# Padding on-chip tiles to 512-byte starts, and weights as the stationary operand in block 1's up projections

## The chip, the cores and the metric

The kernel runs on one core of a Trainium2 chip. The time is the device time of one execution in microseconds (us); the figure that counts is the median over several runs. TensorE (PE in the rows) multiplies: each product first loads a stationary operand of 128x128 numbers (a weight load, PEld in the rows) and then streams a moving operand of up to 512 columns through it into PSUM. VectorE (DVE), ScalarE (ACT) and GpSimd (POOL) do the elementwise work; SyncE (SP) issues the DMAs.

## The reference, cut to what matters

Two transformer-like blocks follow each other on 256 tokens with a width of 1024; a second stream of 256 context tokens joins in the second block.

```python
def swiglu(x, w_gate, w_up, w_down):
    return (jax.nn.silu(x @ w_gate) * (x @ w_up)) @ w_down
...
x = x + 0.5 * swiglu(rmsnorm(x, ffn1_norm[l]), ffn1_w_gate[l], ffn1_w_up[l], ffn1_w_down[l])
x = x + hybrid_mixer(rmsnorm(x, mix_norm[l]), ...)
x = x + 0.5 * swiglu(rmsnorm(x, ffn2_norm[l]), ffn2_w_gate[l], ffn2_w_up[l], ffn2_w_down[l])
...
mods = jnp.split(jax.nn.silu(c) @ w_ada[layer] + b_ada[layer], N_MOD, axis=-1)
h = ffn_sublayer(h, mods[0], mods[1], mods[2], ...)
hc = ffn_sublayer(hc, mods_c[0], mods_c[1], mods_c[2], ...)
...
h = ffn_sublayer(h, mods[6], mods[7], mods[8], ...)
```

The hidden width of every feed-forward part is 2816, which is 22 groups of 128 features. `w_ada` gives the nine modulation vectors of block 2.

## The kernel before, in words

Every float32 factor is split into a high and a low part (`split_out`): ScalarE rounds the high part, VectorE subtracts it from the source for the low part. A product of the reference is three products on TensorE (high x high, high x low, low x high), made by `mm3`, `mm3r`, `projT` or `projT2`, all through `mm` (line 79). So the whole kernel is a stream of about 7,000 products with one weight load each. The splits of a weight go from a tile `raw` (where the DMA lands it) to the tiles `wh` and `wl`; one such unit is 128x1024 numbers, 512 KB. Activations stand transposed in `XH` and `XL` (8 slices of 128 features, 512 tokens each) and hidden activations in slot tiles `S0` to `S17` (`salloc`).

The order of work is one queue per engine. The queues come out of a scheduler that keeps dependences and lets ready work of a later step go ahead; its results are seen in the program's order, shown below for the places of interest.

The four feed-forward parts in the order in which they run:

- Block 1's first and second (`ffn2tok` with `gu1`, `gu2`), on two tiles of 128 tokens. Eleven chunks `c` of 256 features: `proj_chunk` takes the activations as stationary and streams the weights, 512 columns (256 gate, 256 up), 48 products a chunk. `sink_gu` (line 336) makes the gated product on 128 tokens x 256 features; it is then transposed on TensorE (`later`, line 348) so that the down projection can take it as stationary. The RMS factor `r` of a token is a per-partition number here: it goes into the activation's `scale` and into the gated product. The down projection runs over 22 units of `Wd`, 12 products of 512 columns each.
- The context and the tokens of block 2 together (`ffn4tok`, `gu3`, 512 columns): weights stationary, `XH` and `XL` moving; 48 products for each of 22 feature groups, in two parts (12 and 10 groups), each with its down projection.
- Block 2's last (`ffn2tok` with `cols=True`, `gu4`): one chunk in the first form, then for each feature group `f` from 2 to 21 the weights are stationary and 256 columns of `XH` and `XL` move, 48 products a group; no transposes are needed.

Between these lie the two mixers.

Beside the up projections VectorE also makes the row sums of `w_ada` (`ada_gen`, line 543): 72 units of 512 KB are loaded, each is multiplied with `silu(c)` and summed, two such instructions for each of the first 40 units and one for each of the other 32. `self.fill_every` says after how many split units one step of that generator is put into the order.

All tiles lie in one address range of 128 partitions, in the order of the pools. From the sizes in the code the start of each tile within a partition follows; what stands here is its remainder modulo 512 bytes. Slices of a tile that are used as operands begin at multiples of 512 bytes from its start (exceptions: the 272- and 258-column operands of the mixers).

| tile | before | after the change |
|---|---|---|
| `ident` | 128 | 0 |
| `XH`, `XL` | 160 | 0 |
| `t2`, `x2`, `x3`, `bc` | 0 | 0 |
| `S0`, `S1` | 128, 160 | 0 |
| `S2`, `S3` | 192 | 0 |
| `S4` to `S7` | 224 | 0 |
| `S8` to `S12` | 256 | 0 |
| `S13` to `S17` | 288 | 0 |
| `wh`, `wl`, `raw` | 288 | 0 |

In the first part of `ffn4tok`, the first half of the down projection streams `wh` and `wl` against hidden activations in slots. Its third and fourth unit (24 products each) take them from `S13`, `S14`, `S16` and `S17`, the fifth and sixth from `S8` to `S11`.

Of the kernel before, what the change touches and what calls it, by code (L numbers as in the profile page):

```python
# [9 lines left out]
F32 = mybir.dt.float32  # L10
F32R = mybir.dt.float32r
# [12 lines left out]
class Kern:  # L24
    def __init__(self, tc, A, out, pools):
        self.tc, self.nc, self.A, self.out = tc, tc.nc, A, out
        self.__dict__.update(pools)
        self.n = 0
        self.free_slots = list(range(NSLOT))
        self.slot_of = {}  # L30
        self.filler = None
        self.fill_every = 0
        self.fill_count = 0
        self.filled = 0
        self.pre = []
        self.deferred = []
        self.later_pe = []
        self.held = 0


# [10 lines left out]
    def psum(self, tag, shape):  # L51
        return self.ps.tile(shape, F32, tag=tag, name=self.nm(tag), bufs=4)

    def salloc(self, shape, dt=F32):
        i = self.free_slots.pop(0)
        t = self.slots.tile(shape, dt, tag=f"S{i}", name=self.nm(f"S{i}"))
        self.slot_of[id(t)] = (i, t)
        return t
# [262 lines left out]
    def ffn2tok(self, Wgu, Wd, xts, rows, sink, after, skew=4, cols=False, first_by_tile=False, w0=(), fine=False, mid=None, ahead=None):  # L321


        hT = {}

        def dest(f):
# [5 lines left out]
        for c in range(1 if cols else 11):  # L332
            self.fill_every = 2 if self.filler is not None and 1 <= c < 10 else 0
            trs = []

            def sink_gu(t, ps, c=c, trs=trs):
# [4 lines left out]
                if r is None:  # L341
                    self.act(sil, ps[:, :256], AF.Silu)
                    self.tt(h, ps[:, 256:], sil, ALU.mult)
                else:
                    self.act(sil, ps[:, :256], AF.Silu, scale=r)
                    self.stt(h, ps[:, 256:], r, sil, ALU.mult, ALU.mult)

# [17 lines left out]
        if cols:  # L365
            toks = slice(xts[0][0] * P, xts[0][0] * P + 256)
            for f in range(2, NF):
                self.fill_every = 3 if self.filler is not None and f < 20 else 0
                ws = [self.unit(Wgu[2 * f + j]) for j in range(2)]
                pss = [self.psum("acc", [P, 256]) for _ in range(2)]  # L370
                self.projT2(pss, ws, toks)
                sil, h = self.t2([P, 256]), self.t2([P, 256])
                self.act(sil, pss[0], AF.Silu)
                self.tt(h, pss[1], sil, ALU.mult)
                hh, hl, sl = dest(f)
                self.split_out(hh[:, sl, :], hl[:, sl, :], h)
                if f == 2:
                    self.flush()
        if mid is not None:
            mid()  # L380
# [10 lines left out]

        for f in range(NF - skew):
            wh, wl = self.unit(Wd[f])
            hh, hl, sl = dest(f)
# [42 lines left out]
    def ffn4tok(self, Wgu, Wd, xts, sink, after, ws):  # L437

        u0 = 0
        for part, (f0, f1) in enumerate(((0, 12), (12, 22))):  # L440
# [28 lines left out]
            for f in range(f, f1):  # L469
                self.fill_every = 1 if f0 + 4 < f or f0 else 0  # L470
                ws = [self.unit(Wgu[2 * f + j]) for j in range(2)]
                pss = [self.psum("acc", [P, 512]) for _ in range(2)]
                self.projT2(pss, ws, slice(0, 512))
                sink_gu(f, *pss)
            self.fill_every = 0
            nu = (f1 - f0) // 2
            for d in range(2):
                pss = {}

# [624 lines left out]
    def run(self):  # L1104
        nc, A = self.nc, self.A
        x = {}
        for t in (2, 3):
            x[t] = self.xres.tile([P, D], F32, tag=f"x{t}", name=f"x{t}")
        self.ident = self.cpool.tile([P, P], F32, tag="ident", name="ident")
        make_identity(nc, self.ident)  # L1110
        g = {"f1": self.bc.tile([P, D], F32, tag="bc", name="bc_f1")}
# [8 lines left out]
        self.tri = self.cpool.tile([P, 2, P], F32, tag="tri", name="tri")  # L1120
        self.XH = self.cpool.tile([P, 8, 512], F32R, tag="XH", name="XH")
        self.XL = self.cpool.tile([P, 8, 512], F32R, tag="XL", name="XL")
        lat = (2, 3)

        def res_half(t, d, ps):
            s = slice(d * 512, d * 512 + 512)
            self.stt(x[t][:, s], ps, 0.5, x[t][:, s], ALU.mult, ALU.add)

# [29 lines left out]

        self.ffn2tok(A["gu1"], A["d1"], xts, rows, res_half, after)
        g["f2"] = self.bcast(A["ffn2_norm"])  # L1160
# [55 lines left out]

        self.ffn2tok(A["gu2"], A["d2"], xf, rf, res_half, after, mid=mid, ahead=ahead)

# [80 lines left out]
def body(tc, A, out):  # L1299
    with tc.tile_pool(name="const", bufs=1) as cpool, \  # L1300
# [10 lines left out]
        pools = dict(cpool=cpool, xres=xres, small=small, tmp=tmp, bc=bc, rp=rp, slots=slots, raw=raw, wsp=wsp, ps=ps)  # L1311
        k = Kern(tc, A, out, pools)
        k.modd = dram.tile([112, P], F32, tag="modd", name="modd")
        k.mrow = dram.tile([36, 256], F32, tag="mrow", name="mrow")
# [59 lines left out]
def layout(i):  # L1374
# [9 lines left out]
    a["g_final"] = i["g_final_2"].reshape(1, D)  # L1384
    a["gu1"] = pack_gu(i["ffn1_w_gate"][0], i["ffn1_w_up"][0])
    a["gu2"] = pack_gu(i["ffn2_w_gate"][0], i["ffn2_w_up"][0])
    a["gu3"] = pack_T(i["w_ffn1_in_2"][0]).reshape(2, NF, P, D).transpose(1, 0, 2, 3).reshape(2 * NF, P, D)
# [57 lines left out]
```

## Time and profile before

| what | us |
|---|---|
| median of 3 runs | 1427.51 (1427.47 to 1428.04) |
| the profiled execution | 1426.11 |
| its span, first to last instruction | 1424.3 |
| PE busy in it | 1404.2 (99%) |
| DVE busy | 919.5 (65%) |
| ACT busy | 626.5 (44%) |
| mean DMA rate | 183 GB/s |

A busy PE means that some product was in its pipeline at the time; products overlap, so the busy time of one instruction (some 395 ns for 512 columns) is longer than the distance from its start to the next one's. What a product costs is that distance: the difference of two start times divided by the number of products between. In a table of windows the number behind the x also counts instructions that began just before the window, so it is one or two above the number that starts in it.

### The profile page before, as it was taken

What the parts mean: (1) busy time and instruction counts of PE and PEld (TensorE: products, weight loads), DVE (VectorE), ACT (ScalarE), POOL (GpSimd) and SP (SyncE); (2) the same over time, 40 slices, a digit from 0 to 9 for tenths busy, and PEclk for the clock granted to TensorE, in tenths of its full rate; (3) what the DMA queues carried; (4) which work ended last, traced back from release to release, by engine and by line L of the source; (5) the groups of instructions that cost most, each with busy time, mean ns of one, the idle gap of its engine ahead of it and who ended that gap; (6) DMA issues with size and microseconds to landing.
All of it is one profiled execution on the core that took longest, in us unless ns stands there. A gap on an engine that the chain in (4) does not pass through costs nothing. (4 is left out here: it accounts for less than half of the span.)

```text
span 1424.3 us, 18795 instructions
## 1 busy us (share of the span) xinstructions
PE 1404.2 (99%) x7222; PEld 1170.0 (82%) x7222; DVE 919.5 (65%) x1308; ACT 626.5 (44%) x914; POOL 29.3 (2%) x49
## 2 busy tenths in 40 slices
PE   7999999999999999999999999999999999999997
PEld 5888788778888898888888887888988887899986
DVE  5998556878988475542555446476886566655545
ACT  5445447464446442322122224343865455444442
POOL 0000000000000000000000001001010000000000
PEclk9999999999999999999999999999999999999999
DMA  8888646457887664643565442333335666465662
GB/s 278 307 269 275 205 136 204 134 166 259 290 275 254 203 210 132 195 147 102 191 209 178 147 148 94 115 104 129 102 104 187 198 192 206 142 197 179 184 207 69
DMA packets 73307, 260.71 MB, mean 183 GB/s; under 512 B 8172, under 2 KB 9216, under 8 KB 73216
## 3 DMA queue, kind: packets, MB, share of 16 engines
q1 hardware_dynamic: 72928, 259.11, 56.3%
q8 instruction: 57, 0.93, 0.3%
q10 hardware_dynamic: 288, 0.39, 0.1%
q14 instruction: 34, 0.28, 0.1%
HBM read 258.32 MB, written 1.14 MB: 182 GB/s over the span
## 5 line engine op out<-in xcount | busy, mean ns | idle before, releaser
L69 DVE TENSOR_TENSOR wl<-raw,wh 128x1024 fp32r<-128x1024 f32 (+1 forms) x381 | 459.0, 1212 | 330.3 <-ACT wh L66 326.7
L66 ACT ACTIVATE wh<-raw 128x1024 fp32r<-128x1024 f32 (+1 forms) x381 | 398.3, 1049 | 609.0 <-PE acc L79 457.9
L79 PE MATMUL acc<-wh,XH 128*128 128x512 f32 (+2 forms) x816 | 277.3, 398 | 0.4 <-ACT t L66 0.4
L79 PE MATMUL acc<-wh,XL 128*128 128x512 f32 (+2 forms) x816 | 273.4, 393 | 0.2 <-DVE XL L69 0.2
L79 PE MATMUL acc<-wl,XH 128*128 128x512 f32 (+2 forms) x816 | 272.4, 392 | 0.0
L79 PE MATMUL acc<-wh,S 128*128 128x512 f32 x872 | 237.1, 394 | 0.4 <-DVE t L72 0.4
L79 PE MATMUL acc<-XH,wh 128*128 128x512 f32 (+1 forms) x776 | 201.5, 339 | 0.0
L79 PE MATMUL acc<-XH,wl 128*128 128x512 f32 (+1 forms) x776 | 201.2, 339 | 0.0
L79 PE MATMUL acc<-XL,wh 128*128 128x512 f32 (+1 forms) x776 | 201.1, 339 | 0.0
L79 PEld LDWEIGHTS acc<-wh,S 128*128 128x128 f32 x872 | 162.8, 188 | 38.8 <-DVE t L72 1.1
L543 DVE SCALAR_TENSOR_TENSOR S<-raw,S 128x1024 f32<-128x1024 f32 x112 | 136.9, 1222 | 70.6 <-DMA raw<-in_w_ada 69.9
L79 PEld LDWEIGHTS acc<-wh,XL 128*128 128x128 f32 x816 | 152.2, 189 | 34.6 <-DVE XL L69 1.1
L79 PEld LDWEIGHTS acc<-wl,XH 128*128 128x128 f32 x816 | 152.0, 188 | 33.7 <-DVE wl L69 0.3
L79 PEld LDWEIGHTS acc<-wh,XH 128*128 128x128 f32 x816 | 151.7, 189 | 33.9 <-ACT t L66 0.6
L79 PEld LDWEIGHTS acc<-XL,wh 128*128 128x128 f32 x776 | 133.0, 188 | 17.5
L79 PEld LDWEIGHTS acc<-XH,wl 128*128 128x128 f32 x776 | 132.9, 188 | 17.5
L79 PEld LDWEIGHTS acc<-XH,wh 128*128 128x128 f32 x776 | 132.9, 188 | 17.5
L79 PE MATMUL acc<-wl,S 128*128 128x512 f32 x436 | 133.0, 393 | 0.0
L79 PEld LDWEIGHTS acc<-wl,S 128*128 128x128 f32 x436 | 81.9, 188 | 18.4
L66 ACT ACTIVATE S<-t 128x512 fp32r<-128x512 f32 (+2 forms) x58 | 31.4, 542 | 30.2 <-DVE t L69 30.2
L66 ACT ACTIVATE XH<-tr 128x512 fp32r<-128x512 f32 x44 | 26.0, 596 | 41.8 <-PE tr L152 41.3
L152 PE MATMUL tr<-ident,t 128*128 128x128 f32 x200 | 32.1, 285 | 10.4 <-DVE t L69 9.6
(165 smaller groups left out, 892.9 us busy)
## 6 DMA issues: line engine op xcount, KB each, us to landing
raw<-in_gu SPq DMA_DIRECT2D x176, 512.0 KB, 4.4
raw<-in_d SPq DMA_DIRECT2D x88, 512.0 KB, 4.3
raw<-in_w_ada SPq DMA_DIRECT2D x72, 512.0 KB, 4.5
raw<-in_w_in SPq DMA_DIRECT2D x68, 512.0 KB, 4.3
raw<-in_w_qk SPq DMA_DIRECT2D x16, 512.0 KB, 3.5
bc<-modd SPq DMA_DIRECT2D x10, 512.0 KB, 4.4
raw<-in_w_out SPq DMA_DIRECT2D x8, 512.0 KB, 3.5
raw<-in_w_b SPq DMA_DIRECT2D x8, 512.0 KB, 4.3
```

What stands on the lines that cost most here:

```text
L66: return self.nc.scalar.activation(out=out, in_=in_, func=func, **kw)
L69: return self.nc.vector.tensor_tensor(out=out, in0=a, in1=b, op=op)
L79: self.nc.tensor.matmul(out, l, r, start=start, stop=stop, **kw)
L152: self.nc.tensor.transpose(tr[:, j, :], src[:, j * P:(j + 1) * P], self.ident)
L543: nc.vector.scalar_tensor_tensor(out=junk, in0=raw, scalar=1.0, in1=cb[r], op0=ALU.mult, op1=ALU.mult, accum_out=mc[:, o:o + 1])
```

## The change

It has four parts.

1. Pad tiles (`pad`) and a new order of the constant tiles; slot tiles that hold 4x258 numbers take 4608 bytes and not 4128. The table above gives the result.
2. Block 1's two feed-forward parts call `ffn2tok` with `cols=True`, and `layout` packs `gu1` and `gu2` accordingly. Chunk 0 keeps its form; the feature groups 2 to 21 have stationary weights and 256 moving columns. Tokens then lie along the columns, so `r` can no longer be a per-partition factor: four transposes build a tile `R` with `r` of each token in all partitions, VectorE multiplies the gate's sum by `R` ahead of the activation, and the factor of the up half is moved to the residual (`rhalf` is 0.5 times `r`).
3. Where the steps of `ada_gen` go: in block 1's up projections one after 4 units up to group 19 (first) or 15 (second), one after 2 units in the first down projection, and more of them in `ffn4tok`.
4. `res_half` takes `rhalf` in place of 0.5.

```diff
@@ salloc
+        if len(shape) == 3 and shape[1] * shape[2] > D:
+            t = self.slots.tile([P, D + P], dt, tag=f"S{i}", name=self.nm(f"S{i}"))
+            t = t[:, :shape[1] * shape[2]].rearrange("p (a b) -> p a b", a=shape[1])
@@ ffn2tok
+        R = self.salloc([P, 256]) if rows else None
...
-            self.fill_every = 2 if self.filler is not None and 1 <= c < 10 else 0
+            self.fill_every = 0
...
-                    self.stt(h, ps[:, 256:], r, sil, ALU.mult, ALU.mult)
+                    self.tt(h, ps[:, 256:], sil, ALU.mult)
...
+                def row():
+                    tr = self.psum("tr", [P, 256])
+                    for i in range(2):
+                        self.nc.tensor.transpose(tr[:, i * P:i * P + P], b[:, i * P:i * P + P], self.ident)
+                    self.act(R, tr)
+
+                self.after_mm(10, row)
...
-                self.fill_every = 3 if self.filler is not None and f < 20 else 0
+                self.fill_every = 4 if self.filler is not None and f < (16 if mid else 20) else 0
...
-                self.act(sil, pss[0], AF.Silu)
+                if rows:
+                    self.tt(sil, pss[0], R, ALU.mult)
+                    self.act(sil, sil, AF.Silu)
+                else:
+                    self.act(sil, pss[0], AF.Silu)
...
+            self.fill_every = 2 if self.filler is not None and not mid and f < NF - skew - 2 else 0
@@ ffn4tok
-                self.fill_every = 1 if f0 + 4 < f or f0 else 0
+                self.fill_every = 1 if f0 + 2 < f or f0 else 0
+                if f0 and f % 2 and self.filler is not None:
+                    next(self.filler, 0)
...
+                self.fill_every = 0 if part and d else 2
@@ run
+        self.pad(self.cpool, 96)
         self.ident = self.cpool.tile([P, P], F32, tag="ident", name="ident")
+        self.XH = self.cpool.tile([P, 8, 512], F32R, tag="XH", name="XH")
+        self.XL = self.cpool.tile([P, 8, 512], F32R, tag="XL", name="XL")
...
+        self.pad(self.cpool, 32)
...
-            self.stt(x[t][:, s], ps, 0.5, x[t][:, s], ALU.mult, ALU.add)
+            self.stt(x[t][:, s], ps, self.rhalf[t], x[t][:, s], ALU.mult, ALU.add)
...
-        self.ffn2tok(A["gu1"], A["d1"], xts, rows, res_half, after)
+        self.ffn2tok(A["gu1"], A["d1"], xts, rows, res_half, after, cols=True)
...
-        self.ffn2tok(A["gu2"], A["d2"], xf, rf, res_half, after, mid=mid, ahead=ahead)
+        self.ffn2tok(A["gu2"], A["d2"], xf, rf, res_half, after, cols=True, mid=mid, ahead=ahead)
@@ body
+        k.pad(rp, 64)
@@ layout
-    a["gu1"] = pack_gu(i["ffn1_w_gate"][0], i["ffn1_w_up"][0])
-    a["gu2"] = pack_gu(i["ffn2_w_gate"][0], i["ffn2_w_up"][0])
+    a["gu1"] = pack_guT(i["ffn1_w_gate"][0], i["ffn1_w_up"][0])
+    a["gu2"] = pack_guT(i["ffn2_w_gate"][0], i["ffn2_w_up"][0])
```

TensorE's queue in block 1's first up projection, before: the end of one chunk of 256 features, with the transposes (`tr`) of the chunk ahead, and the start of the next. `acc_257` and `acc_258` are the sums of the two token tiles; the operand behind the arrow is the moving one, then the stationary one.

```order
L79 MATMUL acc_258<-wl_304,XH 128x512
L353 MATMUL tr_319<-ident,t_37_238 128x128 x2
L353 MATMUL tr_319<-ident,t_39_248 128x128 x2
L79 MATMUL acc_257<-wh_330,XH 128x512
L79 MATMUL acc_257<-wl_331,XH 128x512
L79 MATMUL acc_257<-wh_330,XL 128x512
L79 MATMUL acc_257<-wh_330,XH 128x512
```

The same queue now, where one feature group ends and the next begins: `acc_368` and `acc_369` are the gate's and the up half's sums over both token tiles.

```order
L88 MATMUL acc_368<-XL,wh_346 128x256
L88 MATMUL acc_369<-XL,wh_352 128x256
L88 MATMUL acc_368<-XH,wl_347 128x256
L88 MATMUL acc_369<-XH,wl_353 128x256
L88 MATMUL acc_437<-XH,wh_427 128x256
L88 MATMUL acc_438<-XH,wh_433 128x256
L88 MATMUL acc_437<-XL,wh_427 128x256
```

Weights and activations have changed places, a product has 256 columns in place of 512, and no transpose stands between two groups.

VectorE's queue in the same up projection, before, for one chunk: four splits (`wl`), the low part of the transposed hidden activations (`S_101`), the two gated products (line 72) and four row sums (line 543).

```order
L69 TENSOR_TENSOR wl_557<-raw_554,wh_556 128x1024
L69 TENSOR_TENSOR S_101_521<-tr_515,S_100_520 128x512
L69 TENSOR_TENSOR wl_577<-raw_574,wh_576 128x1024
L72 SCALAR_TENSOR_TENSOR t_107_541<-acc_461,r_155,t_106_540 128x256
L543 SCALAR_TENSOR_TENSOR S_50_283,mc<-raw_580,S_48_277 128x1024
L72 SCALAR_TENSOR_TENSOR t_109_551<-acc_462,r_166,t_108_550 128x256
L543 SCALAR_TENSOR_TENSOR S_50_283,mc<-raw_580,S_49_280 128x1024
L69 TENSOR_TENSOR wl_599<-raw_596,wh_598 128x1024
L69 TENSOR_TENSOR wl_624<-raw_621,wh_623 128x1024
L543 SCALAR_TENSOR_TENSOR S_50_283,mc<-raw_627,S_48_277 128x1024
L543 SCALAR_TENSOR_TENSOR S_50_283,mc<-raw_627,S_49_280 128x1024
```

The same queue now, for two feature groups, which are as many features as a chunk: `S_31` is `R`, `acc_798` and `acc_867` are the gate's sums of the two groups, `t_140` and `t_150` what goes to the activation, `S_130` the low part of the hidden activations.

```order
L78 TENSOR_TENSOR t_140_848<-acc_798,S_31_184 128x256
L78 TENSOR_TENSOR wl_933<-raw_930,wh_932 128x1024
L78 TENSOR_TENSOR wl_1000<-raw_997,wh_999 128x1024
L78 TENSOR_TENSOR t_141_849<-acc_799,t_140_848 128x256
L78 TENSOR_TENSOR S_130_779<-t_141_849,S_129_778 128x256
L78 TENSOR_TENSOR t_150_917<-acc_867,S_31_184 128x256
L78 TENSOR_TENSOR wl_1006<-raw_1003,wh_1005 128x1024
L78 TENSOR_TENSOR t_151_918<-acc_868,t_150_917 128x256
L78 TENSOR_TENSOR wl_1071<-raw_1068,wh_1070 128x1024
L78 TENSOR_TENSOR S_130_779<-t_151_918,S_129_778 128x256
L577 SCALAR_TENSOR_TENSOR S_69_362,mc<-raw_1080,S_67_356 128x1024
L577 SCALAR_TENSOR_TENSOR S_69_362,mc<-raw_1080,S_68_359 128x1024
```

For the same features there are two row sums in place of four, and two more short instructions that read the gate's sum; one or two splits stand between that instruction and the gated product of the same group.

## Rows read from the trace of the kernel before

**Rows 1.** The page, part 1: busy time, share of the span, instructions.

```profile
span 1424.3 us, 18795 instructions
PE 1404.2 (99%) x7222; PEld 1170.0 (82%) x7222; DVE 919.5 (65%) x1308; ACT 626.5 (44%) x914; POOL 29.3 (2%) x49
```

**Rows 2.** Waits of TensorE: who for whom, us in total, times, longest.

```profile
PE tr L152 <- DVE t L69: 9.6, 3, 6.4
PE tr L152 <- DVE t L72: 0.8, 3, 0.4
```

**Rows 3.** TensorE's timeline in `ffn4tok`'s first down half: start, length, instructions (us).

```profile
657.95 2.00 PE L79 MATMUL acc<-wh,S 128*128 128x512 f32 x8
...
660.69 1.98 PE L79 MATMUL acc<-wh,S 128*128 128x512 f32 x8
...
663.41 1.98 PE L79 MATMUL acc<-wh,S 128*128 128x512 f32 x8
...
666.13 1.98 PE L79 MATMUL acc<-wh,S 128*128 128x512 f32 x8
...
668.86 2.03 PE L79 MATMUL acc<-wh,S 128*128 128x512 f32 x8
...
671.66 2.03 PE L79 MATMUL acc<-wh,S 128*128 128x512 f32 x8
...
674.46 0.39 PE L79 MATMUL acc<-wh,S 128*128 128x512 f32 x1
```

**Rows 4.** The same two stretches as windows: TensorE busy, granted clock, DMA.

```profile
657.95:668.86 10.91, 10.91 (x50) 1.00 0.32 96
668.86:680.06 11.20, 11.20 (x49) 1.00 0.30 94
```

**Rows 5.** Windows: first up projection; `ffn4tok`'s second; last `ffn2tok`'s (PE, PEld, DVE, ACT, POOL, clock, DMA).

```profile
36.00:108.00 72.00, 72.00 (x324) 58.21 (x323) 65.56 (x92) 34.15 (x44) 0.00 (x0) 1.00 0.86 289
713.33:825.32 111.99, 111.99 (x481) 90.10 (x480) 54.75 (x72) 29.67 (x38) 0.00 (x0) 1.00 0.53 172
1246.31:1354.61 108.30, 108.30 (x915) 108.30 (x914) 58.14 (x77) 51.29 (x78) 0.00 (x0) 1.00 0.61 188
```

**Rows 6.** TensorE's timeline around one chunk of the first up projection.

```profile
34.30 0.60 PE L353 MATMUL tr<-ident,t 128*128 128x128 f32 x4
34.65 0.47 PE L79 MATMUL acc<-wh,XH 128*128 128x512 f32 x1
...
45.92 0.60 PE L353 MATMUL tr<-ident,t 128*128 128x128 f32 x4
46.28 0.47 PE L79 MATMUL acc<-wh,XH 128*128 128x512 f32 x1
```

**Rows 7.** TensorE's groups with shapes kept apart: count, busy us, mean ns, idle before.

```profile
L79 PE MATMUL acc<-wh,XH 128*128 128x512 f32 x784 | 271.3, 402 | 0.4 <-ACT t L66 0.4
...
L79 PE MATMUL acc<-wh,S 128*128 128x512 f32 x872 | 237.1, 394 | 0.4 <-DVE t L72 0.4
L79 PE MATMUL acc<-wl,S 128*128 128x512 f32 x436 | 133.0, 393 | 0.0
L79 PE MATMUL acc<-XH,wh 128*128 128x512 f32 x392 | 123.8, 395 | 0.0
...
L79 PE MATMUL acc<-XH,wh 128*128 128x256 f32 x384 | 77.7, 282 | 0.0
```

**Rows 8.** VectorE's and ScalarE's groups, shapes kept apart, same columns.

```profile
L69 DVE TENSOR_TENSOR wl<-raw,wh 128x1024 fp32r<-128x1024 f32 x373 | 453.4, 1222 | 328.4 <-ACT wh L66 326.4 <-PE acc L79 1.0
L543 DVE SCALAR_TENSOR_TENSOR S<-raw,S 128x1024 f32<-128x1024 f32 x112 | 136.9, 1222 | 70.6 <-DMA raw<-in_w_ada 69.9
L543 DVE DVE_READ_ACCUMULATOR S<-raw,S 128x1 f32 x112 | 9.4, 84 | 0.0
L69 DVE TENSOR_TENSOR t<-acc,t 128x256 f32<-128x256 f32 x22 | 9.2, 419 | 1.0 <-ACT t L66 1.0
L66 ACT ACTIVATE t<-acc,r 128x256 f32<-128x256 f32 x46 | 20.3, 468 | 5.0 <-PE acc L79 5.0
```

More of the change, by code (lines that the diff above doesn't have):

```diff
@@ L38, in __init__ @@
         self.held = 0
+        self.rhalf = {}
     def nm(self, s):
@@ L52, in psum, with pad @@
         return self.ps.tile(shape, F32, tag=tag, name=self.nm(tag), bufs=4)
+    def pad(self, pool, n):
+        pool.tile([P, n], F32, tag=f"pad{n}", name=self.nm("pad"), bufs=1)
     def salloc(self, shape, dt=F32):
         i = self.free_slots.pop(0)
-        t = self.slots.tile(shape, dt, tag=f"S{i}", name=self.nm(f"S{i}"))
+        if len(shape) == 3 and shape[1] * shape[2] > D:
+            t = self.slots.tile([P, D + P], dt, tag=f"S{i}", name=self.nm(f"S{i}"))
+            t = t[:, :shape[1] * shape[2]].rearrange("p (a b) -> p a b", a=shape[1])
+        else:
+            t = self.slots.tile(shape, dt, tag=f"S{i}", name=self.nm(f"S{i}"))
         self.slot_of[id(t)] = (i, t)
@@ L366, in ffn2tok @@
             toks = slice(xts[0][0] * P, xts[0][0] * P + 256)
+            if rows:
+                b = self.t2([P, 256])
+                for i, (t, _) in enumerate(xts):
+                    self.ts(b[:, i * P:i * P + P], self.ident, 0.0, rows[t], ALU.mult, ALU.add)
+                    self.rhalf[t] = self.rp.tile([P, 1], F32, tag=f"h{t}", name=self.nm("h"))
+                    self.ts(self.rhalf[t], rows[t], 0.5)
+                def row():
[4 more added lines that the diff above has]
+                self.after_mm(10, row)
             for f in range(2, NF):
-                self.fill_every = 3 if self.filler is not None and f < 20 else 0
+                self.fill_every = 4 if self.filler is not None and f < (16 if mid else 20) else 0
                 ws = [self.unit(Wgu[2 * f + j]) for j in range(2)]
@@ L372, in ffn2tok @@
                 sil, h = self.t2([P, 256]), self.t2([P, 256])
-                self.act(sil, pss[0], AF.Silu)
+                if rows:
+                    self.tt(sil, pss[0], R, ALU.mult)
+                    self.act(sil, sil, AF.Silu)
+                else:
+                    self.act(sil, pss[0], AF.Silu)
                 self.tt(h, pss[1], sil, ALU.mult)
@@ L378, in ffn2tok @@
                     self.flush()
+        if rows:
+            self.sfree(R)
         if mid is not None:
@@ L474, in ffn4tok @@
                 sink_gu(f, *pss)
-            self.fill_every = 0
             nu = (f1 - f0) // 2
             for d in range(2):
+                self.fill_every = 0 if part and d else 2
                 pss = {}
@@ L1120, in run @@
         self.tri = self.cpool.tile([P, 2, P], F32, tag="tri", name="tri")
-        self.XH = self.cpool.tile([P, 8, 512], F32R, tag="XH", name="XH")
-        self.XL = self.cpool.tile([P, 8, 512], F32R, tag="XL", name="XL")
+        self.pad(self.cpool, 32)
         lat = (2, 3)
```

## The prediction

> **What bounds the kernel now.** The page's first part comes first: PE is busy for 99% of the span, VectorE for 65% [rows 1]. That alone proves little, because products overlap; the waits decide. All that TensorE waits for is a handful of moments, 9.6 us of them in three gaps at the start [rows 2]. So the span is about 7,000 products in a row, and the question is the distance from one start to the next.
>
> For 512 columns that distance is not one number. In the first down half of `ffn4tok` twelve products go from 657.95 to 660.69 us, 2.74 us, and again in 2.72, 2.72 and 2.73; from 668.86 on twelve take 2.80, twice [rows 3]. Over 48 products that is 10.91 / 48 = 227.3 ns, and over the next 48 it is 11.20 / 48 = 233.3 ns. [...] What differs is the slots: the fast 48 read stationary operands that begin at 288 bytes modulo 512, as their moving operands do; the slow 48 read them at 256. Elsewhere the two operands stand 128 apart (160 and 288), and there 480 products take 111.99 us, 233.3 ns each [rows 5]; in a chunk of the first up projection 48 take 11.27 us, 234.8 ns [rows 6]. So the distance depends on where operands lie, and equal remainders give the shortest one in this trace.
>
> **The change part by part.** The sum is made against the span of 1424.3 us.
>
> *Padding, 512 columns.* After it all these products have equal remainders (0 and 0), so each gets 227.3 ns, the price of the 48. Of the 4,884 products with 512 columns (the program's count; [rows 7] shows the groups: three of 784, three of 392, 872, 436, and 48 others), 1,056 are block 1's up projections, dealt with below. 1,308 are the down projections with slots (872 + 436): they run between 227.3 and 233.3 already, depending on the slot, so they get half the difference: 1,308 x 3.0 = 3.9 us. The other 2,520 stand 128 apart: 2,520 x 6.0 = 15.1 us. The bound on the other side is zero (rival B); that a start at 0 could be slower than 233.3 I leave out, because no pair of remainders in the trace is much slower than that (234.8 at most, [rows 6]).
>
> [...]
>
> *Padding, 256 columns.* 1,448 such products exist now. 912 of them take 108.30 us, 118.8 ns each [rows 5]; their operands stand 128 apart (160 and 288), and no 256-column product with equal remainders is in the trace. From above the price is 118.8, unchanged. From below: each product has one weight load whatever its width, so if the 6.0 ns belong to the load, 112.8 is left; if they belong to the columns, 118.8 x 227.3 / 233.3 = 115.7. I take 114, between these two and nearer to the first, since it was the stationary operand's place alone that changed within [rows 3]. 1,448 x 4.8 = 6.9 us.
>
> *Block 1's up projections.* A chunk takes 46.28 - 34.65 = 11.63 us, of which the four transposes are 0.36 [rows 6]. Twenty chunks (ten in each part; chunk 0 keeps its form) are 232.6 us. They become 40 groups of 48 products with 256 columns: 40 x 48 x 0.114 = 218.9 us. That saves 13.7 us: 7.2 are the transposes, the rest is what padding does. At the old 118.8 ns it would be 228.1, so 4.5 us saved. The two chunks 0 get 96 x 7.5 ns = 0.7 us. The four transposes for `R` cost 0.4 us.
>
> *VectorE beside it.* Now it is busy for 65.56 of 72 us in that stage [rows 5], 10.6 us of each 11.63. Per group it will do two splits of 1.222 us and three short instructions of 0.42 (product with `R`, gated product, low part) [rows 8]: 3.70 us. A step of `ada_gen` is two row sums, 2 x (1.222 + 0.084) = 2.61 us, once in two groups: 5.01 us against 48 x 0.114 = 5.47 of TensorE. I cost the new instruction at nothing, since this slack covers it; without the cover, 40 x 0.42 = 17 us. What is queued behind the multiplication with `R` when it waits for the gate's sum are the splits for later groups and the row sums. They are two groups ahead (five pairs of `wh` and `wl`), so a wait there reaches TensorE only after some 5 us.
>
> *Where the row sums go.* The first down projection gets one step after two units: 1.222 + 1.31 = 2.53 us of VectorE for 12 products, 2.73 us. That is 93%, and the cover is thin, but the up projections run at 91% now without TensorE waiting. Its DMA is 1.5 x 524 KB in 2.73 us, 288 GB/s, and 289 are carried in the up projection now at a share of 0.86 [rows 5]. In `ffn4tok` a group takes 10.9 us, and VectorE is busy for only 54.75 of 112 [rows 5]. These moves cost nothing. Nor do `rhalf` in place of 0.5 and the pads.
>
> Sum: 3.9 + 15.1 + 6.9 + 13.7 + 0.7 - 0.4 = 39.9 us. The span becomes 1384.4. The profiled execution took 1426.11 us, 1.8 above its span, and the median of the runs is 1427.51, 1.4 above that: 1427.5 - 39.9 = 1387.6, so 1388 us, 2.8% faster.
>
> **The rivals.**
>
> *A: the start address itself counts too.* The fast 48 have equal remainders, but their operands still cross a 512-byte boundary inside each slice; after the change none does. [...] Against it: operands with the same difference but other places cost about the same (chunks at 288 and 160, groups at 160 and 288, within 1.5 ns).
>
> [...]
>
> *B: the padding does not do what the 48 suggest.* The 227.3 could come from those slots or from that stretch, say from how the halves alternate. Then only the new form of the up projections counts: 4.5 - 0.4 = 4.1 us, 1423.4 us. For it: only a few hundred products show the short distance. Against it: the two stretches follow each other without a pause.
>
> *C: slower.* TensorE comes to wait for VectorE in block 1's up projections. There are two pairs of accumulators; if the chain from the gate's sum (product with `R` 0.42, activation 0.47, gated product 0.42 [rows 8]) is held up behind splits and row sums so that it lies open in each group, that is 1.31 x 40 = 52 us: 1388 + 52 = 1440. It decides from 43 us, 1.07 us a group, that is from 6.5 us of VectorE's time per group where I count 5.01. A group with a step of `ada_gen` has 6.31, but its neighbour has 3.70. In the trace's own groups of this form, VectorE is busy 58.14 of 108.30 us and nothing waits [rows 2, 5].
>
> **How the numbers follow.** My forecast 58%, A 25%, B 10%, C 4%, and 3% for losses that eat up most of the gain. The likeliest case has its own range by the price of 256 columns: at 118.8 the sum is 23.8 (1404), at 112.8 it is 43.9 (1384). The range for 8 in 10 reaches into A and ends short of B: 1332 to 1420; left out are A's lower part (about 7%), B's upper half and C. About 0.2%, 3 us, is what a measurement of this kernel can tell from no change. Faster by more than that are my forecast, A and most of B: 0.91; within it 0.04; slower 0.05.
>
> **What will show it.** [...] A group in block 1's up projections should take 5.47 us from its first product to the next group's; if it is longer, and TensorE's waits name VectorE or ScalarE in that stage, C is at work. VectorE's share in windows of that stage should be near 92%. The prediction is wrong if 512 columns do not come to one distance, or if 256 columns keep 118.8.

## The result and the profile after

| | before | after |
|---|---|---|
| median of 4 runs each, us | 1427.49 (1427.29 to 1428.04) | 1411.70 (1411.19 to 1411.89) |
| ratio, 95% interval | | 0.9888 [0.9871, 0.9905] |
| span of the profiled execution, us | 1424.3 | 1410.0 |

The kernel became 1.1% faster, 15.8 us; 39.9 were forecast. The page's first part, as [rows 1]:

```profile
span 1410.0 us, 20702 instructions
PE 1386.7 (98%) x8106; PEld 1213.3 (86%) x8106; DVE 936.5 (66%) x1376; ACT 628.0 (45%) x936; POOL 29.3 (2%) x49
```

TensorE has 884 products more and still nearly no pause. Its waits, as [rows 2]:

```profile
PE tr L161 <- DVE t L78: 10.0, 3, 7.1
PE tr L161 <- DVE t L81: 2.1, 4, 1.1
PE acc L88 <- ACT t L75: 0.9, 1, 0.9
PE acc L88 <- DVE t L78: 0.8, 1, 0.8
...
PE tr L388 <- DVE t L85: 0.4, 1, 0.4
```

All lines of this view add up to 15.2 us (11.9 before). So the loss against the forecast is again in the distance between starts. In the first down half of `ffn4tok`, as [rows 3]:

```profile
647.08 1.98 PE L88 MATMUL acc<-wh,S 128*128 128x512 f32 x8
...
649.80 1.98 PE L88 MATMUL acc<-wh,S 128*128 128x512 f32 x8
...
652.52 1.98 PE L88 MATMUL acc<-wh,S 128*128 128x512 f32 x8
...
655.24 1.98 PE L88 MATMUL acc<-wh,S 128*128 128x512 f32 x8
...
657.96 1.98 PE L88 MATMUL acc<-wh,S 128*128 128x512 f32 x8
```

Twelve products of 512 columns take 2.72 us each time, 226.7 ns a product. The padding does for 512 columns what the fast 48 products of [rows 3] promised. Three windows, with the columns of [rows 5] (the first up projection, a stretch of 381 products of 512 columns in the second mixer, the last `ffn2tok`):

```profile
36.00:108.00 72.00, 72.00 (x603) 72.00 (x602) 59.41 (x91) 33.73 (x49) 0.00 (x0) 1.00 0.77 253
881.39:967.73 86.34, 86.34 (x383) 71.33 (x382) 47.19 (x71) 33.78 (x46) 2.88 (x2) 1.00 0.34 111
1231.42:1340.82 109.40, 109.40 (x915) 109.40 (x913) 58.12 (x77) 51.14 (x77) 0.00 (x0) 1.00 0.58 186
```

The second is 86.34 / 380 = 227.2 ns from start to start. The third holds the same 912 products of 256 columns as before, and they take 109.40 / 911 = 120.1 ns, where the kernel before had 108.30 us and 118.8. Here the padding made them slower, and the forecast had 114. In the first window 600 products begin in 72 us, 120.0 ns each (a few of the 603 records began ahead of it): block 1's new form pays the same price, 40 groups of 48 at 120.0 = 230.4 us for the 232.6 of the twenty chunks [rows 6].

TensorE's groups (as [rows 7]) show how much hangs on it: of 256 columns there are now 3,368 (the 1,448 of before and 1,920 in block 1's up projections), most of them in these three.

```profile
L88 PE MATMUL acc<-XH,wh 128*128 128x256 f32 x1024 | 207.4, 283 | 0.0
L88 PE MATMUL acc<-XL,wh 128*128 128x256 f32 x1024 | 207.1, 283 | 0.0
L88 PE MATMUL acc<-XH,wl 128*128 128x256 f32 x1024 | 207.0, 283 | 0.0
```

Their mean of one (283 ns, 282 before) says nothing: it is the length of a product that overlaps the next ones. Only the starts show the price.

### The profile page after: what moved, and what is told of

It reads as the page before. It is cut to its first block, busy times and chain, and to the rows that moved or that the text cites. A ratio compares the mean times of both kernels' runs of the same rounds, so it can differ in the third digit from the quotient of the medians.

```text
span 1410.0 us, 20702 instructions
## 1 busy us (share of the span) xinstructions
PE 1386.7 (98%) x8106; PEld 1213.3 (86%) x8106; DVE 936.5 (66%) x1376; ACT 628.0 (45%) x936; POOL 29.3 (2%) x49
## 5 line engine op out<-in xcount | busy, mean ns | idle before, releaser
L88 PE MATMUL acc<-XH,wh 128*128 128x256 f32 (+1 forms) x1416 | 328.9, 313 | 0.0
L88 PE MATMUL acc<-XL,wh 128*128 128x256 f32 (+1 forms) x1416 | 328.4, 312 | 0.0
L88 PE MATMUL acc<-XH,wl 128*128 128x256 f32 (+1 forms) x1416 | 328.4, 312 | 0.0
L88 PEld LDWEIGHTS acc<-XH,wh 128*128 128x128 f32 x1416 | 233.5, 191 | 15.7
L88 PEld LDWEIGHTS acc<-XH,wl 128*128 128x128 f32 x1416 | 233.6, 191 | 15.3
L88 PEld LDWEIGHTS acc<-XL,wh 128*128 128x128 f32 x1416 | 233.6, 191 | 15.2
L88 PE MATMUL acc<-wh,XH 128*128 128x512 f32 (+1 forms) x496 | 166.7, 393 | 0.9 <-ACT t L75 0.9
L88 PE MATMUL acc<-wh,XL 128*128 128x512 f32 (+1 forms) x496 | 164.2, 387 | 0.2 <-DVE XL L78 0.2
L88 PE MATMUL acc<-wl,XH 128*128 128x512 f32 (+1 forms) x496 | 163.0, 386 | 0.0
L88 PEld LDWEIGHTS acc<-wh,XH 128*128 128x128 f32 x496 | 91.3, 189 | 19.1 <-ACT t L75 1.1
```

The lines of the kernel that those rows point to most:

```text
L88: self.nc.tensor.matmul(out, l, r, start=start, stop=stop, **kw)
```

## The experiments

Theory R: the distance of two products depends on the difference of the two operands' starts modulo 512 bytes (moving minus stationary), by a curve that is another one for each width; a difference of 0 is the best for 512 columns and the worst for 256. The rivals: the 512-byte boundary itself counts, or the form rather than the padding carried the gain, or VectorE sets the pace of the new form.

**Padding alone, form alone, everything shifted by 128 bytes.** The first leaves out the new form and the moved row sums, the second leaves out the padding, the third changes one pad of the changed kernel.

```diff
@@ padding alone, as against the changed kernel (gu2 likewise; the rest of parts 2 to 4 of the change goes too) @@
-        self.ffn2tok(A["gu1"], A["d1"], xts, rows, res_half, after, cols=True)
+        self.ffn2tok(A["gu1"], A["d1"], xts, rows, res_half, after)
@@ form alone @@
-            t = self.slots.tile([P, D + P], dt, tag=f"S{i}", name=self.nm(f"S{i}"))
...
-        self.pad(self.cpool, 96)
@@ all shifted by 128 bytes @@
-        self.pad(self.cpool, 96)
+        self.pad(self.cpool, 128)
```

> The kernel before with the padding alone; block 1's up projections keep the 512-column form with its row sums. Theory R (256 columns cost 120.0 ns at equal remainders, 512 cost 227): the new form is worth less than nothing, 40 groups of 48 at 120.0 = 230.4 us against 20 chunks at 48 x 227 + 0.36 ns = 225.1 us, so this kernel is faster than the changed one by about 5 us: 1404 to 1408 us. The prediction's prices (114 ns for 256 columns) with the measured 1411.7: the new form gains some 6 us more at equal remainders, so this kernel would be slower than the changed one, about 1418 us.

> The changed kernel without the padding: the tiles stand at remainders 128 to 288 as before. Theory R: 512 columns back at 232 to 233 ns, 256 columns at 118.6 to 118.8, so the new form gives 20 chunks at 11.63 = 232.6 against 40 groups at 48 x 118.8 = 228.1 us, less about 2 us of new stalls: 1423 to 1426 us. If the form rather than the padding carried the gain, this kernel would stand at about 1412 us.

> The changed kernel with every operand of the products 128 bytes behind a multiple of 512, so that all remainders are equal but none is zero. Theory R (the difference counts): 1411.7 us, no change from the changed kernel, 512 columns at 227 ns. Rival (multiples of 512 themselves count): 512 columns back at about 233 ns, 3,924 x 6 ns = 23 us lost, about 1430 us.

| kernel | us | ratio to before |
|---|---|---|
| padding alone | 1411.35 | 0.9885 [0.9871, 0.9898] |
| form alone | 1425.81 | 0.9983 [0.9974, 0.9992] |
| all shifted by 128 bytes | 1414.49 | 0.9903 [0.9888, 0.9918] |

The padding alone gives the whole gain (1428.20 us for the kernel before in that round), the form alone 2.4 us; that settles the second rival. Windows of the form alone, of its first up projection and of the 381 products:

```profile
32.00:140.18 108.18, 108.18 (x915) 108.18 (x912) 88.69 (x135) 52.92 (x77) 0.00 (x0) 1.00 0.75 247
889.20:977.83 88.63, 88.63 (x383) 71.45 (x382) 47.28 (x71) 33.81 (x46) 2.74 (x3) 1.00 0.34 109
```

Without padding 256 columns are back at 108.18 / 911 = 118.7 ns, 512 at 88.63 / 380 = 233.2. The kernel with everything shifted, the 381 products and the last up projection:

```profile
884.49:970.89 86.40, 86.40 (x384) 71.34 (x382) 47.21 (x71) 33.80 (x46) 2.88 (x2) 1.00 0.33 111
1234.18:1343.58 109.40, 109.40 (x915) 109.40 (x913) 58.12 (x77) 51.13 (x77) 0.00 (x0) 1.00 0.59 187
```

Though every operand now begins 128 bytes behind a multiple of 512, these are the windows of the changed kernel: 227.4 and 120.1 ns. So the difference counts and the boundary does not. Its 2.8 us more are not in the steady distances. Of TensorE's waits in its trace, one is new, of 1.1 us in `ffn4tok` at 709.6 us; the waits together are 16.3 us (15.2 in the changed kernel). Where the rest of the 2.8 us lies stays open.

```profile
PE acc L88 <- ACT wh L75: 1.1, 1, 1.1
```

That the padding alone is no faster than the changed kernel was not expected: 1404 to 1408 was. More of it at the end of this section.

**A bench of the distance.** 51 settings of 48 products each behind the last product of the changed kernel, one after another; the core of it:

```diff
+            q = self.ps.tile([P, 512], F32, tag="tr", name=nm, bufs=4)
+            for j in range(48):
+                k = j % 7
...
+                    w = (wh, wl)[j % 2]
...
+                    l, r = w[:, k * P + so:k * P + so + m], xf[:, k * 512 + o:k * 512 + o + n]
+                self.nc.tensor.matmul(q[:m, :n], l, r, start=j == 0, stop=j == 47)
```

> The changed kernel with a bench of 48 products per setting behind its last product (its outputs are computed as before; the bench's sums go nowhere). Theory R (only the start of the streamed operand minus the start of the weights, modulo 512 bytes, sets the distance): 512 columns 227 ns at difference 0, 229 at 64, 233 at 128, and the same again at difference 0 when both operands start 128 bytes behind a multiple of 512; 256 columns 120.0 ns at difference 0 and about 118.6 at 128. [...] The price taken in the prediction, 114 ns for 256 columns, would have to show at some difference if it exists at all. Rival (the 512-byte boundary itself counts): with both operands 128 bytes off, 512 columns go back to about 233 ns.

TensorE's timeline of the bench; each pair is two products of one setting that lie 24 distances apart. `qaa` is 512 columns at difference 0, `qaf` at 128, `qbg` at 0 with both operands 128 bytes off; `qal` 256 columns at 0, `qap` at 64; `qbx` and `qby` are all 48 products of 512 and of 256 columns in bfloat16. The granted clock is 1.00, and the rest of the core is nearly idle (from 1405 to 1822 us VectorE is busy for 3.5 us, ScalarE for 28.3, the DMA's share is 0.01).

```profile
1407.38 0.39 PE L1165 MATMUL qaa<-XH,wl 128*128 128x512 f32 x1
...
1412.82 0.39 PE L1165 MATMUL qaa<-XH,wl 128*128 128x512 f32 x1
...
1462.60 0.39 PE L1165 MATMUL qaf<-XH,wh 128*128 128x512 f32 x1
...
1468.17 0.40 PE L1165 MATMUL qaf<-XH,wh 128*128 128x512 f32 x1
...
1528.44 0.28 PE L1165 MATMUL qal<-XH,wl 128*128 128x256 f32 x1
...
1531.32 0.28 PE L1165 MATMUL qal<-XH,wl 128*128 128x256 f32 x1
...
1551.11 0.28 PE L1165 MATMUL qap<-XH,wl 128*128 128x256 f32 x1
...
1553.83 0.28 PE L1165 MATMUL qap<-XH,wl 128*128 128x256 f32 x1
...
1663.53 0.39 PE L1165 MATMUL qbg<-XH,wl 128*128 128x512 f32 x1
...
1668.97 0.39 PE L1165 MATMUL qbg<-XH,wl 128*128 128x512 f32 x1
...
1805.38 10.53 PE L1165 MATMUL qbx<-xb,wb 128*128 128x512 bf16 x48
1815.75 5.40 PE L1165 MATMUL qby<-xb,wb 128*128 128x256 bf16 x48
```

5.44 / 24 = 226.7, 5.57 / 24 = 232.1, 2.88 / 24 = 120.0, 2.72 / 24 = 113.3 and again 226.7 ns. (The 5.40 us of `qby` contain the length of its last product; its starts are 5.13 us apart, 5.13 / 47 = 109.2 ns.) From the 11th start to the 48th of each setting, for all differences (ns):

| difference, bytes | 0 | 8 | 16 | 32 | 64 | 128 | 192 | 256 | 320 | 384 | 448 |
|---|---|---|---|---|---|---|---|---|---|---|---|
| 512 columns | 226.7 | 233.4 | 231.7 | 233.3 | 228.9 | 232.3 | 233.4 | 226.7 | 228.8 | 232.3 | 233.3 |
| 256 columns | 120.0 | 120.0 | 116.7 | 116.8 | 113.3 | 118.6 | 113.3 | 120.0 | 117.8 | 118.8 | 113.3 |

Theory R's curve is there: 0 and 256 are best for 512 columns and, with 8, worst for 256. With both operands 128 bytes off, 256 columns are at 120.0 as well, and 512 columns with the weights alone 128 bytes off (difference 384) at the same 232.3 as with the moving operand 384 bytes off. At difference 0, 320 and 384 columns take 146.7 and 173.4 ns and lie with the 120.0 of 256 and the 226.7 of 512 on one line: 64 columns more cost 26.7 ns, and drawn on to no columns the line leaves 13.3 ns. But a fixed price for a load of weights is not what that is: 128 and 192 columns both take 111.7 where the line has 66.7 and 93.3, 448 take 202.6 instead of 200.0, the same weights over and over cost as much as changing ones (226.7 and 120.0), and narrower weights (32, 64, 96 columns) cost more at 512 columns, 229.9 to 231.6, and less at 256, 113.3 to 116.0. Why the curve has this shape no run shows.

**The weights of the 256-column products moved by 64 bytes.** To leave the 512-column products at 0, both halves of a unit share one tile, and only the stationary-weight loops of `ffn2tok` write them 64 bytes further on.

```diff
-            wh = self.wsp.tile([P, 1024], F32R, tag="wh", name=self.nm("wh"))
-            wl = self.wsp.tile([P, 1024], F32R, tag="wl", name=self.nm("wl"))
+            w = self.wsp.tile([P, 2176], F32R, tag="w", name=self.nm("w"))
+            wh, wl = w[:, off:off + 1024], w[:, off + 1024:off + 2048]
...
-                ws = [self.unit(Wgu[2 * f + j]) for j in range(2)]
+                ws = [self.unit(Wgu[2 * f + j], 16) for j in range(2)]
```

> The changed kernel with the weights of the 2,880 products of 256 columns in the three stationary-weight up loops written 64 bytes further on (both halves in one tile of 8,704 bytes, all other operands still at equal remainders). The bench showed 113.3 ns for 256 columns when the streamed operand starts 64 bytes before the weights (difference 448), against 120.0 at equal remainders. Theory R: 2,880 x 6.7 ns = 19.2 us less, about 1392 us, and the new form then beats the old one. Rival (VectorE, which splits the weights, paces these loops at the present rate, or the bench does not hold beside other traffic): 1405 to 1412 us, with waits for VectorE in block 1.

> The kernel with both halves of the weights in one tile of 8,704 bytes, but without the shift of 64 bytes: all operands of the products at equal remainders. If the shift made the 15.9 us, this kernel stands with the changed one, 1410 to 1414 us. Rival (the one tile instead of two made some of it): below 1408 us.

With the shift 1395.72 us, ratio 0.9771 [0.9757, 0.9784]; with the one tile alone 1409.10, 0.9866 [0.9851, 0.9881]. The one tile brought 2.6 us by the medians, but the intervals of its ratio and of the changed kernel's ([0.9871, 0.9905]) overlap, so this is not clear of the spread; it was not expected and is not explained. The shift brought 13.4. The first loop in the kernel with the shift, the second up to 396.86 us, and the third:

```profile
32.01:139.39 107.38, 107.38 (x915) 107.38 (x913) 88.49 (x133) 53.11 (x77) 0.00 (x0) 1.00 0.74 248
331.60:396.86 65.26, 65.26 (x578) 65.26 (x577) 55.58 (x86) 33.12 (x49) 0.00 (x0) 1.00 0.71 231
1222.01:1325.36 103.35, 103.35 (x915) 103.35 (x914) 59.90 (x77) 49.42 (x77) 0.00 (x0) 1.00 0.62 195
```

The first is 107.38 / 911 = 117.9 ns, the second 65.26 / 575 = 113.5, the third 103.35 / 911 = 113.4, with the same difference and the same order of products. In its trace TensorE waits for nothing between 30 and 140 us, and VectorE is at least as busy beside the fast second stretch (55.58 of 65.26 us) as beside the slow first (88.49 of 107.38), so the third rival falls too.

**Two rhythms at one difference.** A second bench: the order of products of an up group (48 products, two units), each difference begun in five ways; and, in the kernel, the shift by 448 and by 320 bytes (differences 64 and 192). A rhythm here is a distance that lasts through a whole setting or loop.

```diff
+            if p:
+                n = (0, 320, 448, 288, 256)[p]
+                r = z[:, :n] if p == 4 else xs[0][:, :n]
+                self.nc.tensor.matmul(q[:, :n], us[0][0][:, :P], r, start=True, stop=True)
...
@@ the two other shifts @@
-                ws = [self.unit(Wgu[2 * f + j], 16) for j in range(2)]
+                ws = [self.unit(Wgu[2 * f + j], 112) for j in range(2)]
...
+                ws = [self.unit(Wgu[2 * f + j], 80) for j in range(2)]
```

> The changed kernel with a second bench behind its last product (its outputs are computed as before): the order of products of an up group at 256 columns, 48 products per setting, at 8 differences between streamed operand and weights, each begun in five ways (straight on; after one product of 320, 448 or 288 columns; after a wait of TensorE). Theory S (at one difference there can be more than one lasting rhythm, and how the group begins picks it): at 448, where the kernel with shifted weights showed 117.8 in one loop and 113.3 in another, the five beginnings give both. At 0 it is 120.0 for all five. Rival (the rhythm belongs to the difference and the buffers): the same distance for all five beginnings at each difference.

> As the kernel with weights shifted by 64 bytes, but by 448 (difference 64). The shift by 64 brought 15.9 us, with 1,400 of 2,880 products at 117.8 ns and the others at 113.3. Theory S with a rhythm of 113.3 whenever the loop falls into it: between 1390 us (all at 113.3) and 1398 us (all at 117.8). Rival (only the difference 448 works): 1411 us.

> As the kernel with weights shifted by 64 bytes, but by 320 (difference 192, where the bench showed 113.3 ns). Theory S: 1390 to 1398 us. Rival: 1411 us.

Its timeline at difference 64, after one product of 320 columns (`qab`) and after one of 448 (`qac`); 24 distances lie between the row of `qab` and the next, and between the second row of `qac` and that of `qad`:

```profile
1414.07 0.39 PE L1160 MATMUL qab<-XH,wh 128*128 128x256 f32 x2
...
1416.79 0.36 PE L1152 MATMUL qac<-XH,wh 128*128 128x448 f32 x1
...
1419.82 0.40 PE L1160 MATMUL qac<-XH,wh 128*128 128x256 f32 x2
...
1422.65 0.29 PE L1152 MATMUL qad<-XH,wh 128*128 128x288 f32 x1
```

2.72 / 24 = 113.3 and 2.83 / 24 = 117.9 ns: the same operands, another beginning, and each rhythm lasts. Over the five beginnings difference 64 gave 113.3 twice and 117.8 three times, 192 gave 113.3 three times and 117.8 twice, 448 always 113.3, 320 always 117.8, 0 always 120.0 (and 16 gave 116.7 twice and 118.7 three times, so the table above has one rhythm of each; for 512 columns this was not tried). So theory S holds, though not at the difference that it named: at 448 the bench did not show the 117.8 that the kernel's first loop had. The kernels with the two other shifts took 1400.17 us (0.9821 [0.9808, 0.9835]) and 1396.08 (0.9780 [0.9761, 0.9798]), the first outside the range expected; its runs lie between 1396.7 and 1405.0. In its profiled execution, the fastest, the first loop ran at 113.3 and the last at 117.9 ns. That the wider spread is the rhythm falling out differently is a guess, since only one execution of each has a trace.

Within a loop the switch can be seen. The second loop of the kernel with the shift by 64 bytes has one transpose of another step in it, of the row sums' results `mc`; the window behind it:

```profile
396.98 0.27 PE L585 MATMUL tr<-ident,mc 128*48 128x128 f32 x1
...
397.32:436.43 39.11, 39.11 (x335) 39.11 (x333) 26.08 (x37) 19.33 (x29) 0.00 (x0) 1.00 0.74 245
```

Ahead of this one product the distance is 113.5 ns, behind it 39.11 / 332 = 117.8 to the end of the loop, and TensorE waits for nothing there. VectorE is less busy beside this slower end (26.08 of 39.11 us) than beside the faster part ahead of it. The kernels with the two other shifts have the same transpose at 393.44 and 396.13 us, and in both 113.3 turns into 117.8 there. This also accounts for the 13.4 us of the shift by 64: some 1,350 products at 117.8 and some 1,530 at 113.4 in place of 120.0 are about 13 us.

**Is the new form worth what the prediction said, at the price that it took?** The padding and the old form, with the shift in the last block alone.

```diff
@@ on the padding alone, with the one tile @@
-                ws = [self.unit(Wgu[2 * f + j]) for j in range(2)]
+                ws = [self.unit(Wgu[2 * f + j], 16) for j in range(2)]
```

> The padding with the old form of block 1's up projections, and the shift of 64 bytes (in the one tile) for the 960 products of 256 columns of the last block alone, the only loop of that form in it. At 113.3 to 117.8 instead of 120.0 ns they bring 2 to 6.4 us: 1405 to 1410 us. Against the kernel with the new form and the shift (1395.7) the new form is then worth 9 to 14 us, as the prediction had it (13.7) for 256 columns at 114 ns. Rival (the new form is worth nothing even at the better price): about 1396 us.

1405.90 us, 0.9849 [0.9827, 0.9871]. Against 1395.72 the new form, with its moved row sums, is worth 10.2 us by the medians once its columns cost 113.4 to 117.9; at 120.0 it was worth nothing (1411.35 against 1411.70). The 10.2 are not sharp: the runs lie between 1402.8 and 1408.3 on one side and 1392.8 and 1396.1 on the other. The spans of the two profiled executions, 1401.0 and 1394.3, differ by 6.7 us, and 5.7 of them lie in block 1's two up projections.

**Row sums and the old form.** At 120.0 ns the old form should have won by about 5 us. A clean chunk of the padding alone does take less than two groups (11.37 against 96 x 120.0 ns = 11.52 us), but not all are clean. The transposes between its chunks:

```profile
34.24 0.60 PE L361 MATMUL tr<-ident,t 128*128 128x128 f32 x4
...
45.61 0.60 PE L361 MATMUL tr<-ident,t 128*128 128x128 f32 x4
...
56.97 0.60 PE L361 MATMUL tr<-ident,t 128*128 128x128 f32 x4
...
69.24 0.60 PE L361 MATMUL tr<-ident,t 128*128 128x128 f32 x4
...
81.04 0.60 PE L361 MATMUL tr<-ident,t 128*128 128x128 f32 x4
```

11.37, 11.36, then 12.27 and 11.80 us. Counting only distances that are over 20 ns too long, the padding alone loses 5.6 us between 40 and 160 us of its span, the changed kernel 1.1. Theory V puts these gaps down to VectorE, which is late with splits and gated products because of the row sums. Three kernels with other numbers of row sums:

```diff
@@ padding alone, half of the sums; the others beside down products (and in `ffn4tok` as in the change) @@
-            self.fill_every = 2 if self.filler is not None and 1 <= c < 10 else 0
+            self.fill_every = 4 if self.filler is not None and 1 <= c < 10 else 0
...
+            self.fill_every = 2 if self.filler is not None and not mid and f < NF - skew - 2 else 0
@@ changed kernel, more sums; none beside block 1's down products @@
-                self.fill_every = 4 if self.filler is not None and f < (16 if mid else 20) else 0
+                self.fill_every = 2 if self.filler is not None and f < 20 else 0
...
-            self.fill_every = 2 if self.filler is not None and not mid and f < NF - skew - 2 else 0
@@ padding alone, a sum at every third split @@
-            self.fill_every = 2 if self.filler is not None and 1 <= c < 10 else 0
+            self.fill_every = 3 if self.filler is not None and 1 <= c < 10 else 0
```

> The padding with the old form of block 1's up projections, but with half as many row sums beside them, the others beside the down products and the later up projections as in the changed kernel. Theory V (in the padded kernel of the old form VectorE was late at the first up projections, 65 us busy of 72, and products left gaps of some 5 us between 36 and 160 us): these gaps go, about 1406 us, some 5 us faster than the padding alone. Rival (the gaps come from something that the row sums do not set): 1411 us as the padding alone.

> The changed kernel with the row sums beside block 1's up projections as many as in the kernel before, and none beside block 1's down products. Theory V: VectorE has about as much to do in an up pair as in the old form (a group also takes its gate product's row factor, 84 ns more of multiplying per group, no longer both products), so some 3 to 5 us of gaps come back: 1414 to 1418 us. Rival (the number of row sums does not matter in the new form, their move was worth nothing): 1411 to 1412 us.

> The padding with the old form, with a row sum at every third split of weights beside block 1's up projections and none beside its down products. The fewer-sums kernel removed the gaps between 40 and 120 us (3.4 to 0.7 us) but lost 7.7 us at once where row sums beside the down products waited for their weights. Theory V (VectorE's and the queue's load sets the gaps): gaps of 40 to 160 us fall from 5.6 to about 1 us without the new loss, 1406 to 1408 us, which would make the old form with padding faster than the changed kernel. Rival: 1411 us or more.

They took 1412.77 (0.9890 [0.9874, 0.9906]), 1419.79 (0.9945 [0.9933, 0.9958]) and 1416.98 us (0.9930 [0.9918, 0.9943]). All three lie outside what was expected by theory V (about 1406, 1414 to 1418, 1406 to 1408). More row sums beside the new form cost 8.1 us: the fewer row sums of the change are what its form needs. The first window as above shows it (the kernel with more sums: 578 records, VectorE 68.06 of 72 us; the changed kernel: 603 and 59.41):

```profile
36.00:108.00 72.00, 70.95 (x578) 69.53 (x577) 68.06 (x108) 33.50 (x48) 0.00 (x0) 1.00 0.84 272
```

Fewer beside the old form removed the gaps there as theory V says (0.7 us between 40 and 120 us instead of 3.4; with the third, 1.0 between 40 and 160) but not on the whole. By the starts, block 1's two up projections with their transposes take 252.7 and 252.8 us in these two, 257.9 in the padding alone and 258.5 in the changed kernel: in that stage the old form does win by 5 to 6 us. It is lost again in the other products of 512 columns, whose starts add up to 891.4 and 893.8 us for 884.2 in the padding alone. With half the sums one wait of 5.1 us came at the first down products, and with the third 6.9 us of gaps came between 400 and 480 us. The wait, in the kernel with half the sums (120 to 160 us):

```profile
PE acc L87 <- DVE t L80: 5.1, 1, 5.1
```

So for the old form no arrangement was found that beats the changed kernel. Whether VectorE or the arrival of weights sets the gaps stays open: between 36 and 160 us ScalarE's splits wait 49.4 us for `in_gu` in the padding alone (31.6 in the new form with more sums, 1.1 in the changed kernel), and both kinds of load fall when row sums move.

## Why the prediction was off

**The step that failed** is the price of 256 columns: "I take 114, between these two", with bounds of 112.8 and 118.8. At equal remainders it is 120.0, outside both. 3,368 products x 6.0 ns = 20.2 us, of 25.6 that the span fell short (39.9 forecast, 14.3 measured). The reasoning behind it was that what is good for 512 columns could only be good, or indifferent, for 256. No row of before had 256 columns at equal remainders, and a price without a row needs a bound on the losing side too. The distances from each product to the next, added up in the two profiled executions, show where the gain is missing:

| part | forecast, us | measured, us |
|---|---|---|
| 512 columns outside block 1's up projections (3,828) | -19.0 | 899.7 to 883.8: -15.9 |
| 256 columns that stood before (1,448) | -6.9 | 173.0 to 176.4: +3.4 |
| block 1's two up projections, with chunk 0 and transposes | -14.0 | 259.1 to 258.5: -0.6 |
| all else | 0 | -1.2 |

Of the +3.4, the price makes 1,448 x 1.2 = 1.7 and one wait 1.1. In the up projections 1,920 x 6.0 = 11.5 of the missing 13.4 are the price.

**512 columns.** The price was right, 226.7 to 227.2 ns for 227.3, in every stage that was looked at, in down halves whatever the slot. The terms of 3.9 and 15.1 us came to 15.9, pauses behind such products included. Without distances of 260 ns and more, the down products went from 230.7 to 227.1 ns (3.6 where 3.0 were taken), the others from about 232.7 to 227.1 (5.6 where 6.0 were taken): the 2,520 had not all been at 233.3 (the bench has 232.3 at 128).

**The rest.** TensorE's waits grew by 3.3 us [rows 2], 1.3 of them for `t` from L81 and 0.5 for `t` of ScalarE at 217.9 us, in the mixer. (In the kernel before, two of the three gaps of 9.6 us stand at the start; the third, of 0.2 us, at 1205 us.) Rival C did not come: in both up projections the groups' products wait for nothing, the transposes for `R` wait 0.4 us, and the first down product, at 144.2 us, 0.8 for 0.4 before. VectorE was busy for 59.41 of 72 us there, 83% and not 92%: a group took 5.76 us and not 5.47, and VectorE's work in it was 4.75 and not 5.01. But the cover was thin, as the prediction said of the down projection: with more row sums beside the up projections, the kernel lost 8.1 us.

**The rivals.** A is out: a start at a multiple of 512 is worth nothing of its own (226.7 and 120.0 ns in the bench, with both operands there and with both 128 bytes behind it). The lower end of the range, 1332 us, rests on shorter distances in case A, which no run shows: the shortest for 512 columns of float32r was 226.7 ns. B is out: the padding did for all 512-column products what the 48 showed. No rival had a price above 118.8 for 256 columns. That 1411.7 us lies in the range of 1332 to 1420 is luck: with 256 columns at 118.8, their dearest price, the forecast gave 1404, and the range went beyond that for rival B and for losses elsewhere.

What in the chip makes the distance differ no run shows. With all else nearly idle, it differs in the bench by up to 6.7 ns with the difference of the two operands' starts (226.7 to 233.4 ns for 512 columns, 113.3 to 120.0 for 256). The bfloat16 products in a row take 215.8 ns for 512 columns and 109.2 for 256, 11 ns less than the float32r products at difference 0.

**What the mechanism was worth.** That stationary weights and 256 columns can save time in block 1 was right, and its size wrong: at equal remainders they saved nothing, and with weights at the difference where 256 columns take 113.3 to 117.9 ns the form brings 7 to 10 us where 13.7 were forecast. That kernel, at 1395.72, beats both kernels.

## What to carry to other kernels

Where TensorE hardly ever waits, measure the distance of starts for each width and each difference of operand starts before laying out tiles; one rule of alignment for all widths can help one and harm the other (here 226.7 ns for 512 columns, from 233.3, and 120.0 for 256, from 118.8, at the same difference). A price that the trace doesn't have is to be measured by a few dozen products behind the kernel's end rather than put between two neighbours. Work that fills idle engines and is moved away from one stage lands in another: look at what waits there (here 7 to 10 us came back).

## What the runs showed of the hardware that was not expected

- The distance of float32r products depends on moving start minus stationary start modulo 512 bytes, not on either alone (226.7 and 120.0 ns with both at 0 or both at 128 bytes), and by another curve for 256 columns than for 512 (table above).
- At one difference there can be two lasting rhythms, 113.3 and 117.8 ns for 256 columns, and the products ahead of the loop pick one (difference 64: two of five beginnings against three). One transpose in the middle of a loop turned 113.5 into 117.8 ns.
- At difference 0, 128 and 192 columns cost the same, 111.7 ns: from 192 down to 128 nothing is gained, and against the 113.3 to 120.0 of 256 columns, by their difference, between 1.6 and 8.3 ns.
- In bfloat16, 512 and 256 columns take 215.8 and 109.2 ns, with differences of 0 and 256 bytes mixed; whether the difference of starts matters there was not tried.
